# A two-layer encoder trunk on one core: x and mem also loaded transposed, the first norm scaled in after the first projection, keys and values of mem in one projection

## The chip, the cores and the metric

One core of a Trainium2 chip. The time is device microseconds (us) for one execution, as the median of several. The engines are named as the profile names them: PE is TensorE (PEld its weight loads), ACT is ScalarE, DVE is VectorE, POOL is GpSimd, SP is SyncE, which here issues every DMA, so that SP's order is the order of all loads.

## The reference

x is 256 tokens by 1024 features, mem is 256 by 1024, all f32. There are two layers, each a feed-forward block (FFN), a mixing block and a second FFN:

```python
h = rms_norm(x, ffn1_pre_g[l])
x = x + 0.5 * rms_norm(swiglu(h, ffn1_w_up[l], ffn1_w_down[l]), ffn1_post_g[l])
h = rms_norm(x, mix_pre_g[l])
u_pool, q_da, k_da, v_da, q_ca = jnp.split(h @ w_in[l], IN_SPLITS, axis=-1)
...
kv = rms_norm(mem, mem_norm_g[l]) @ w_mem_kv[l]
y_ca = memory_cross_attention(q_ca, kv)
...
x = x + rms_norm(merged @ w_out[l], mix_post_g[l])
h = rms_norm(x, ffn2_pre_g[l])
x = x + 0.5 * rms_norm(swiglu(h, ffn2_w_up[l], ffn2_w_down[l]), ffn2_post_g[l])
```

`rms_norm` divides each token's row by the root of its mean square and multiplies by a gain per feature; `swiglu` is `(silu(a) * b) @ w_down` with `a, b` the halves of `h @ w_up`. Each w_up has 2 x 2816 columns, each w_mem_kv 512 (256 for keys, 256 for values).

## The kernel before, in words

**Numbers.** A product in f32 is made of three matmuls on a split of each operand: a high part (fp32r, the rounded cast, on ACT) and a low part (the rest, on DVE). `mm3` (L201 to 209) issues high x high, high x low, low x high for each 128 features. Weights come as *units* of 128 x 2048 f32 (1 MiB). `load_unit` issues a unit's DMA into one of 3 raw buffers; `next_unit` (L105) casts it (ACT, L115) and makes its low part (DVE, L116) into one of 5 buffers. The first 5 units of a stage are split in 4 parts, later ones in 2.

**Tokens.** Two chunks c of 128 tokens. Activations that are multiplied stand transposed (features on partitions) in a tile `xhl`, high and low. `pre_norm` (L159) makes them: squares on ACT (L141) with a sum, DVE adds (L143), POOL raises to the power -0.5 (L134), DVE scales by 1/rms and gain, PE transposes eight 128 x 128 blocks (L182), ACT and DVE split them (L149, L150).

**An FFN** (L269) runs over 11 pairs of 256 hidden columns. Pairs 0 and 1 take the *wide* form: `up` with tokens as the stationary operand, 24 matmuls of 512 columns per chunk, then silu (L300), the product (L302), and two transposes per chunk (L307), which stand behind the next chunk's matmuls. Pairs 2 to 10 take the *narrow* form, `up2` (L314), with weights as the stationary operand; its result is already transposed, so it has no transposes. After pair p the down projection of pair p-2 follows (L249). Two units feed one wide pair, two feed one narrow pair, one feeds a down projection.

**Start of the program** (L713 to 727): load x chunk 0, the gain, unit 0, x chunk 1, units 1 and 2; 18 matmuls on zeros (`WARM`, L725); then `pre_norm` of chunk 0 with its transposes and of chunk 1; its transposes are placed behind the 20th matmul of the first `up`. The first FFN takes `(c, p)` in the order (0,0), (1,0), (0,1), (1,1).

**Memory tokens.** In the first FFN of each layer, after pair 4, `mem_norm` (L454) loads mem and normalizes it; its 16 transposes come with pair 6. In the mixing block keys are made by `form_a` (weights stationary) and values by `form_b` (tokens stationary), 48 matmuls of 256 columns each.

**Order.** The program is scheduled by the tile framework, in the order of the code with priorities by dependence; `issue_after` pins a few places, and the tables `T_...` tell which matmul of the mixing block's running list an attention step follows.

Of the kernel before, what the change touches and what calls it, by code (L numbers as in the profile page):

```python
# [17 lines left out]
P = 128  # L18
D = 1024
KT = D // P  # L20
S = 256
# [9 lines left out]
WARM = 18  # L31
T_FIRST = 19
# [4 lines left out]
T_DA = (275, 298, 341, 356)  # L37
T_PV = (282, 306, 349, 371)
T_LN = (321, 392)
T_CA = (412, 438)  # L40
T_CAV = (432, 442)
# [5 lines left out]
def encoder_kernel(ctx, tc, x_d, mem_d, pos_d, w_d, gains_d, cols_d, lamv_d, poolw_d, cst_d, out_d):  # L47
# [44 lines left out]
    first_xn = []  # L92
# [11 lines left out]
    def next_unit():  # L104
# [8 lines left out]
        for s in range(parts):  # L113
            cs = slice(s * n, (s + 1) * n)
            nc.scalar.copy(out=h[:, cs], in_=raw[:, cs])  # L115
            low = nc.vector.tensor_tensor(out=l[:, cs], in0=raw[:, cs], in1=h.bitcast(F32)[:, cs], op=ALU.subtract)  # L116
            if nxt[1] == 0:
                issue_after([low], first_xn[1])
# [13 lines left out]
    def rsqrt(v, n):  # L132
        r = sm(n)
        nc.gpsimd.tensor_tensor(out=r, in0=v, in1=mhalf[:, :n], op=ALU.pow)  # L134
        return r

    def rstd_of(halves, fold=1.0, between=None):
        s = sm(2)
        for i, h in enumerate(halves):
            junk = small.tile([P, 512], BF16, name="junk", bufs=2)  # L140
            nc.scalar.activation(out=junk, in_=h, func=AF.Square, scale=fold / 32.0, accum_out=s[:, i:i + 1])  # L141
# [4 lines left out]
        return rsqrt(v, 1)  # L146

    def split(ps, h, l):
        nc.scalar.copy(out=h, in_=ps)  # L149
        nc.vector.tensor_tensor(out=l, in0=ps, in1=h.bitcast(F32), op=ALU.subtract)  # L150
# [8 lines left out]
    def pre_norm(c, src, g, xx, direct=None):  # L159
# [8 lines left out]
        r = rstd_of(src, 1.0, None if direct else gained)  # L168
        for b in range(2):
            fs = slice(b * 512, (b + 1) * 512)  # L170
            if direct:
                first_xn.append(nc.vector.scalar_tensor_tensor(out=xn[:, fs], in0=src[b], scalar=r, in1=direct[b], op0=ALU.mult, op1=ALU.mult))
            else:
                nc.vector.tensor_scalar(out=xn[:, fs], in0=xn[:, fs], scalar1=r, scalar2=None, op0=ALU.mult)
# [26 lines left out]
    def mm3(out, pairs):  # L201
# [3 lines left out]
        for (ah, al), (bh, bl) in pairs:  # L205
            for lhsT, rhs in ((ah, bh), (ah, bl), (al, bh)):
                done.append(nc.tensor.matmul(out=out, lhsT=lhsT, rhs=rhs, start=(i == 0), stop=(i == n - 1)))  # L207
# [23 lines left out]

    def form_b2(out, lo, hi, c, xx):
        pairs = []
        for i, w in enumerate((lo, hi)):
            wh, wl = (t.rearrange("p (k m) -> p k m", k=4) for t in w)
            pairs += [((xx[0][:, c, 4 * i + k, :], xx[1][:, c, 4 * i + k, :]), (wh[:, k, :], wl[:, k, :])) for k in range(4)]
        return mm3(out, pairs)
# [31 lines left out]
    def ffn(i, xx, late, g_post, finish, ahead):  # L269
# [25 lines left out]
        def up(p, c, ws):  # L295
            ps = ma_bank()
            now = form_b2(ps, ws[0], ws[1], c, xx)
            flush()
            sg = t2((P, 2, P))
            nc.scalar.activation(out=sg, in_=ps[:, 0:256].rearrange("p (u m) -> p u m", u=2), func=AF.Silu)  # L300
            hn = t2((P, 2, P))
            nc.vector.tensor_tensor(out=hn, in0=ps[:, 256:512].rearrange("p (u m) -> p u m", u=2), in1=sg, op=ALU.mult)  # L302
# [9 lines left out]
            return now  # L312
# [16 lines left out]
        ws = [(next_unit(), next_unit()) for _ in range(2)]  # L329
        for p in range(2):  # L330
            hid_pair(p)
        done = []
        order = [(0, 0), (0, 1), (1, 0), (1, 1)] if i > 0 else [(0, 0), (1, 0), (0, 1), (1, 1)]
        for c, p in order:
            now = up(p, c, ws[p])
            done += now
            if len(done) == (48 if i > 0 else 24):
                issue_after(late, done[T_UP if i > 0 else T_FIRST])
        for p in range(2, NPR):
            hid_pair(p)  # L340
            for u in range(2):
                up2(p, u)
            if p - 2 <= NPR - 4:
                down(p - 2)
            if p == 4:
                turns = ahead()
            if p == 6:
                for t in turns:
                    t()
# [4 lines left out]
    colt = const.tile([P, DEPTH * 3], F32, name="colt")  # L354
# [8 lines left out]
    def setup():  # L363
        nc.sync.dma_start(out=cst, in_=cst_d)
        nc.sync.dma_start(out=colt, in_=cols_d)
# [70 lines left out]
    def lambdas():  # L436
        nc.scalar.activation(out=lamt, in_=lams, func=AF.Exp)
        for l in range(DEPTH):
            nc.vector.tensor_scalar(out=lamc[:, l:l + 1], in0=lamt[:, 2 * l:2 * l + 1], scalar1=lamt[:, 2 * l + 1:2 * l + 2],
                                    scalar2=lam_init[l], op0=ALU.subtract, op1=ALU.add)  # L440
            nc.vector.tensor_scalar(out=gsub[:, l:l + 1], in0=colt[:, l * 3 + 2:l * 3 + 3], scalar1=1.0 - lam_init[l], scalar2=None, op0=ALU.mult)
# [12 lines left out]
    def mem_norm(l):  # L454
        g = gain(l * 10 + 3)
        mm = xt_pair()
        turns = []
        for c in range(2):
# [5 lines left out]
            turns.append(pre_norm(c, m, g, mm))  # L464
        return mm, turns

    def mix(l, xx, late, mm, finish):
# [71 lines left out]
        w = next_unit()  # L539
        ps = ma_bank()  # L540
        for t in range(2):
            fill += form_a(ps[:, t * S:(t + 1) * S], w, slice(t * P, (t + 1) * P), mm)
        nc.scalar.copy(out=kc.rearrange("p t s -> p (t s)"), in_=ps)
        w = next_unit()
        ps = ma_bank()
        for c in range(2):
            fill += form_b(ps[:, c * 256:(c + 1) * 256], w, c, mm)
        nc.scalar.copy(out=vc.rearrange("p c m -> p (c m)"), in_=ps)
# [174 lines left out]
    wb = mb_bank()  # L723
    for _ in range(WARM):
        nc.tensor.matmul(out=wb, lhsT=warm[:, 0:P], rhs=warm, start=True, stop=True)  # L725
    pre_norm(0, halves(x[0]), None, cur, g0)()
    late = pre_norm(1, halves(x[1]), None, cur, g0)()
# [133 lines left out]
```

## Time and profile before

| what | value |
|---|---|
| median of 3 runs | 1154.98 us (1154.05 to 1155.45) |
| the profiled execution, span from first to last instruction | 1154.1 us |
| PE busy | 1141.8 us, 99% of the span |
| DVE, ACT, POOL busy | 768.6, 634.1, 28.6 us |
| DMA | 217.82 MB, 189 GB/s over the span |

The span is what the profile gives as this execution's own time; it is 0.9 us under the median of the runs. The profile names an instruction by its engine, its line in the kernel, what it writes and reads, and the number of instructions in a group. The chain of waits goes back from the last instruction to what released each step, so a stretch of it that is all PE is one in which PE alone sets the pace.

### The profile page before, as it was taken

How to read it: one execution, taken by the hardware profiler on the slowest of the kernel's cores; microseconds unless marked ns; L12 is line 12 of the kernel's file. 1: busy time of each engine (PE TensorE's matmuls, PEld its weight loads, DVE VectorE, ACT ScalarE, POOL GpSimd, SP SyncE). 2: the span in 40 equal slices, each digit the busy share in tenths (PEclk: the TensorE clock that was granted, in tenths of full speed). 3: DMA queues.
4: the chain of work that ended last, by engine and by line, in shares of the span. 5: the costliest groups of instructions: out<-in, count | busy, mean ns of one | idle time of the engine just before them, and what ended most of it. 6: DMA issues, size and time to landing. Idle time of an engine off the chain costs nothing.

```text
span 1154.1 us, 15241 instructions
## 1 busy us (share of the span) xinstructions
PE 1141.8 (99%) x5930; PEld 963.4 (83%) x5930; DVE 768.6 (67%) x1198; ACT 634.1 (55%) x1141; POOL 28.6 (2%) x39
## 2 busy tenths in 40 slices
PE   8999999999999999999999999999999999999997
PEld 5888888898888888888888888888978888888886
DVE  5768665665767876665586766675677678666653
ACT  5657554644665555555465655556455646555551
POOL 0000000000000100000000000010000001000000
PEclk8999999999999999999999999999999999999999
DMA  8865554564444575555456665535535544755530
GB/s 298 299 236 213 183 183 146 183 219 146 164 172 162 194 271 191 183 182 189 176 191 228 223 216 180 185 141 192 209 120 194 201 165 166 248 190 182 183 110 36
DMA packets 34055, 217.82 MB, mean 189 GB/s; under 512 B 4032, under 2 KB 4288, under 8 KB 9664
## 3 DMA queue, kind: packets, MB, share of 16 engines
q1 hardware_dynamic: 33984, 216.86, 53.0%
q8 instruction: 46, 0.75, 0.3%
q14 instruction: 25, 0.20, 0.0%
HBM read 215.80 MB, written 1.05 MB: 188 GB/s over the span
## 4 chain that ended last, share of the span: by engine, by line
PE 98%; DMA 1%; ACT 0%; SPq 0%; issue 0%; DVE 0%; DVEq 0%; POOLq 0%; ACTq 0%
PE ma L207 30%; PE acc L249 25%; PE mb L226 18%; PE ma L226 18%; PE mb L207 2%; PE mb L182 1%; PE acc L207 1%; PE acc L560 1%; DMA raw<-in_w 1%; PE mb L449 1%; PE acc L577 1%; PE acc L618 1%; PE acc L603 1%; PE mb L307 0%; PE mb L691 0%; PE mb L507 0%
## 5 line engine op out<-in xcount | busy, mean ns | idle before, releaser
L116 DVE TENSOR_TENSOR wl<-raw,wh 128x1024 fp32r<-128x1024 f32 (+1 forms) x444 | 460.2, 1077 | 140.2 <-ACT wh L115 125.9
L115 ACT CAST wh<-raw 128x1024 fp32r<-128x1024 f32 (+1 forms) x444 | 392.1, 935 | 169.8 <-issue 112.4
L207 PE MATMUL ma<-wh,xhl 128*128 128x512 f32 (+1 forms) x928 | 290.5, 390 | 1.9 <-ACT xhl L149 1.9
L249 PE MATMUL acc<-wh,hid 128*128 128x512 f32 x704 | 223.8, 390 | 0.0
L226 PE MATMUL ma<-xhl,wh 128*128 128x512 f32 x576 | 209.9, 399 | 0.0
L226 PE MATMUL mb<-xhl,wh 128*128 128x512 f32 x576 | 209.3, 398 | 0.0
L207 PEld LDWEIGHTS ma<-wh,xhl 128*128 128x128 f32 x928 | 172.8, 190 | 37.5 <-ACT xhl L149 2.2
L207 PE MATMUL ma<-wl,xhl 128*128 128x512 f32 (+1 forms) x464 | 180.2, 388 | 0.0
L249 PEld LDWEIGHTS acc<-wh,hid 128*128 128x128 f32 x704 | 132.2, 188 | 26.1
L226 PE MATMUL ma<-xhl,wl 128*128 128x256 f32 x576 | 150.1, 281 | 0.0
L226 PE MATMUL mb<-xhl,wl 128*128 128x256 f32 x576 | 150.1, 281 | 0.0
L249 PE MATMUL acc<-wl,hid 128*128 128x512 f32 x352 | 137.1, 389 | 0.0
L226 PEld LDWEIGHTS ma<-xhl,wh 128*128 128x128 f32 x576 | 108.2, 188 | 20.9
L226 PEld LDWEIGHTS mb<-xhl,wh 128*128 128x128 f32 x576 | 108.7, 189 | 19.2
L324 DVE TENSOR_TENSOR s<-mb,s 128x256 f32<-128x256 f32 x72 | 30.6, 425 | 130.2 <-ACT s L323 130.1
L226 PEld LDWEIGHTS mb<-xhl,wl 128*128 128x128 f32 x576 | 109.0, 189 | 6.6
L226 PEld LDWEIGHTS ma<-xhl,wl 128*128 128x128 f32 x576 | 108.8, 189 | 5.9
L207 PEld LDWEIGHTS ma<-wl,xhl 128*128 128x128 f32 x464 | 88.2, 190 | 17.3 <-issue 1.3
L249 PEld LDWEIGHTS acc<-wl,hid 128*128 128x128 f32 x352 | 66.2, 188 | 13.9
L325 ACT ACTIVATE s<-s 128x256 f32<-128x256 f32 x72 | 30.1, 418 | 69.5 <-DVE s L324 69.5
L323 ACT COPY s<-mb 128x256 f32<-128x256 f32 x72 | 26.8, 372 | 74.3 <-PE mb L226 74.3
L134 POOL TENSOR_TENSOR sm<-sm,mhalf 128x1 f32<-128x1 f32 (+1 forms) x32 | 27.9, 871 | 1119.8 <-DVE sm L143 855.2
(153 smaller groups left out, 991.3 us busy)
## 6 DMA issues: line engine op xcount, KB each, us to landing
raw<-in_w SPq DMA_DIRECT2D x190, 1024.0 KB, 4.9
gain<-in_gains SPq DMA_DIRECT2D x20, 512.0 KB, 5.2
raw<-in_w SPq DMA_DIRECT2D x4, 512.0 KB, 8.3
hid<-in_mem SPq DMA_DIRECT2D x8, 256.0 KB, 6.0
x<-in_x SPq DMA_DIRECT2D x4, 256.0 KB, 6.3
out<-x SPq DMA_DIRECT2D x4, 256.0 KB, 2.1
cst<-in_cst SPq DMA_DIRECT2D x1, 304.0 KB, 5.3
pw<-in_poolw SPq DMA_DIRECT2D x2, 128.0 KB, 4.0
```

What stands on the lines that cost most here:

```text
L115: nc.scalar.copy(out=h[:, cs], in_=raw[:, cs])
L116: low = nc.vector.tensor_tensor(out=l[:, cs], in0=raw[:, cs], in1=h.bitcast(F32)[:, cs], op=ALU.subtract)
L134: nc.gpsimd.tensor_tensor(out=r, in0=v, in1=mhalf[:, :n], op=ALU.pow)
L182: tps.append(nc.tensor.transpose(out=ps[:, k * P:(k + 1) * P], in_=xn[:, i * P:(i + 1) * P], identity=ident))
L207: done.append(nc.tensor.matmul(out=out, lhsT=lhsT, rhs=rhs, start=(i == 0), stop=(i == n - 1)))
L226: nc.tensor.matmul(out=o, lhsT=ww[:, k, ms], rhs=rhs, start=(k == 0 and o is full), stop=(k == KT - 1 and o is full))
L249: done.append(nc.tensor.matmul(out=banks[b], lhsT=a, rhs=ww[:, k, fs], start=(kk == first and k == 0 and i == 0), stop=(kk == last and k = ...
L323: nc.scalar.copy(out=half, in_=banks[i][:, S:2 * S])
L324: nc.vector.tensor_tensor(out=half, in0=banks[i][:, 0:S], in1=half, op=ALU.add)
L325: nc.scalar.activation(out=t[:, 0:S], in_=t[:, 0:S], func=AF.Silu)
L449: ins.append(nc.tensor.transpose(out=tp[:, i * P:(i + 1) * P], in_=a[:, hh, kt * P:(kt + 1) * P], identity=ident))
L560: nc.tensor.matmul(out=banks[m][:, hh * S:(hh + 1) * S], lhsT=qT[rs, c, 2 * hp + hh, :], rhs=kT[rs, :, 2 * hp + hh, :], start=True, stop=True)
```

## The change

The host also gives x and mem transposed. The first FFN of layer 0 splits raw x^T, times the gain, straight from the load (no norm, no transposes ahead of its matmuls); 1/rms of each token, computed beside, is applied where the projection is read out of PSUM, in silu's scale and in the product. That needs tokens on partitions, so all 11 pairs of this FFN take the wide form. mem^T times its gain is split in the same way; 1/rms of mem is computed once, for both layers, and applied where the keys and values are read out. Keys and values are one wide projection, and the keys are transposed afterwards, two blocks per chunk.

```diff
-WARM = 18
+WARM = 11
...
-T_DA = (275, 298, 341, 356)
+T_DA = (227, 250, 293, 308)
...
+    def gained_split(out, src, col):
+        high = nc.scalar.activation(out=out[0], in_=src, func=AF.Copy, scale=col)
+        return high, nc.vector.scalar_tensor_tensor(out=out[1], in0=src, scalar=col, in1=out[0].bitcast(F32), op0=ALU.mult, op1=ALU.subtract)
...
+        def up_first(p, ws):
+            banks = [ma_bank(), ma_bank()]
+            for i, w in enumerate(ws):
+                for c in range(2):
+                    mm3(banks[c], half_b(w, i, c, xx), i == 0, i == 1)
+            for c in range(2):
+                swiglu(p, c, banks[c])
...
+            if raw_rstd:
+                nc.scalar.activation(out=sg, in_=gate, func=AF.Silu, scale=raw_rstd[c])
+                nc.vector.scalar_tensor_tensor(out=hn, in0=value, scalar=raw_rstd[c], in1=sg, op0=ALU.mult, op1=ALU.mult)
...
+        if raw_rstd:
+            hs, ls = first_high, first_low
+            (ha, la), (hb, lb), (hc, lc), (hd, ld) = (zip(*late[c, b]) for b in range(2) for c in range(2))
+            in_order([*ha, *hs[0:4], *hb, *hc, hs[4], hs[5], *hd, *hs[6:8]])
+            in_order([*la, *ls[0:4], *lb, *lc, ls[4], ls[5], *ld, *ls[6:8]])
+            ws.append((next_unit(), next_unit()))
+            for c in range(2):
+                rstd_of(halves(x[c]), 1.0, None, raw_rstd[c])
...
-            for u in range(2):
-                up2(p, u)
+            if raw_rstd:
+                w2 = (next_unit(), next_unit())
+                for c in range(2):
+                    up(p, c, w2)
+            else:
+                for u in range(2):
+                    up2(p, u)
...
-    def mem_norm(l):
...
+    def mem_gain(l):
+        mm = xt_pair()
+        for b in range(4):
+            t = hids.tile([P, 2, 2, P], F32, name="hid")
+            nc.sync.dma_start(out=t, in_=memt_d[:, b * 512:(b + 1) * 512].rearrange("p (k c t) -> p k c t", k=2, c=2))
+            for i in range(2):
...
+                gained_split((mm[0][:, :, k, :], mm[1][:, :, k, :]), t[:, i], colt[:, col:col + 1])
...
-            fill += form_a(ps[:, t * S:(t + 1) * S], w, slice(t * P, (t + 1) * P), mm)
-        nc.scalar.copy(out=kc.rearrange("p t s -> p (t s)"), in_=ps)
...
+            now = form_b2(ps, ws[0], ws[1], c, mm)
...
+            nc.scalar.activation(out=kt.rearrange("p t d -> p (t d)"), in_=ps[:, 0:S], func=AF.Copy, scale=rmem[:, c:c + 1])
+            nc.vector.tensor_scalar(out=vc[:, c, :], in0=ps[:, S:2 * S], scalar1=rmem[:, c:c + 1], scalar2=None, op0=ALU.mult)
...
-    load_x(0)
-    g0 = halves(gain(0))
-    load_unit(2)
-    load_x(1)
-    load_unit(2)
-    load_unit()
+    xt = {(0, 0): load_tokens(0, 0)}
+    nc.sync.dma_start(out=colt, in_=cols_d)
+    load_unit(4)
+    xt[1, 0] = load_tokens(1, 0)
+    xt[0, 1] = load_tokens(0, 1)
+    load_unit(4)
+    xt[1, 1] = load_tokens(1, 1)
+    load_unit(2)
+    for c in range(2):
+        load_x(c)
```

`half_b` is one unit's half of `form_b2`; `mem_scale` (once) loads mem and computes its 1/rms.

The change moves instructions at the start. ACT before, from its first instruction (`s_271` and `s_305` are silu's outputs, `hid<-mb` the first split of the hidden tile):

```order
1 L413 ACT_TABLE_LOAD
2 L413 ACTIVATE sm<-mhalf 128x1
3 L141 ACTIVATE junk,sm<-x_91 128x512 x2
4 L115 CAST wh<-raw 128x512 x4
5 L149 CAST xhl<-mb 128x512 x2
6 L141 ACTIVATE junk,sm<-x_92 128x512 x2
7 L115 CAST wh<-raw 128x512 x6
8 L149 CAST xhl<-mb 128x512 x2
9 L115 CAST wh<-raw 128x512 x2
10 L300 ACTIVATE s_271<-ma 128x256
```

and ACT now, from the same place (`hid<-in_xt` tiles hold x^T, `rst` is 1/rms):

```order
3 L165 ACTIVATE xhl<-hid,colt 128x128 x4
4 L114 CAST wh<-raw 128x512 x4
5 L165 ACTIVATE xhl<-hid,colt 128x128 x8
6 L114 CAST wh<-raw 128x512 x2
7 L165 ACTIVATE xhl<-hid,colt 128x128 x4
8 L114 CAST wh<-raw 128x512 x6
9 L145 ACTIVATE junk,sm<-x_91 128x512 x2
10 L145 ACTIVATE junk,sm<-x_92 128x512
11 L330 ACTIVATE s_299<-ma,rst 128x256
12 L145 ACTIVATE junk,sm<-x_92 128x512
13 L330 ACTIVATE s_303<-ma,rst 128x256
14 L154 CAST hid<-mb 128x256 x2
```

The squares of x moved from ahead of every weight cast to behind the casts of units 0, 1 and 2, and no split waits for a transpose any more. All of this feeds from SP, whose first rows now are these (20 DMAs stand ahead of unit 3, which is the first of those of `128x2048`; `x_91` and `x_92` are the two chunks of x):

```order
1 L170 DMA hid<-in_xt 128x512
2 L773 DMA colt<-in_cols 128x30
3 L99 DMA raw<-in_w 128x512 x4
4 L170 DMA hid<-in_xt 128x512 x2
5 L99 DMA raw<-in_w 128x512 x4
6 L170 DMA hid<-in_xt 128x512
7 L99 DMA raw<-in_w 128x1024 x2
8 L83 DMA x_91<-in_x 128x512 x2
9 L83 DMA x_92<-in_x 128x512 x2
10 L87 DMA gain<-in_gains 128x1024
11 L99 DMA raw<-in_w 128x2048 x10
```

Before, x and the gain came first, and units 0 to 2 in five pieces; what moved is that x now lands behind unit 2. The third place is ACT around the memory tokens in the first FFN, now (`lamt`, `snd` and `csd` are small constants; `s_881` is silu's output for chunk 0 of pair 5):

```order
40 L145 ACTIVATE junk,sm<-hid 128x512 x2
41 L482 ACT_TABLE_LOAD
42 L482 ACTIVATE lamt<-lams 128x4
43 L145 ACTIVATE junk,sm<-hid 128x512 x2
44 L165 ACTIVATE xhl<-hid,colt 128x2x128
45 L451 ACT_TABLE_LOAD
46 L451 ACTIVATE snd<-turns 128x2x8
47 L452 ACTIVATE snd<-turns 128x2x8
49 L165 ACTIVATE xhl<-hid,colt 128x2x128 x7
50 L154 CAST hid<-mb 128x256
51 L330 ACT_TABLE_LOAD
52 L330 ACTIVATE s_881<-ma,rst 128x256
```

Before, the four squares and the table loads there stood between weight casts and silus; now they and the eight splits of mem^T stand in one piece ahead of pair 5's silu.

## Rows read from the trace of the kernel before

**Rows 1.** The page: busy time by engine, and the granted clock in 40 slices.

```profile
PE 1141.8 (99%) x5930; PEld 963.4 (83%) x5930; DVE 768.6 (67%) x1198; ACT 634.1 (55%) x1141; POOL 28.6 (2%) x39
...
PEclk8999999999999999999999999999999999999999
```

**Rows 2.** The chain of waits, 0 to 60 us: start, us, what.

```profile
2.59 8.47 DMA raw<-in_w
...
12.75 7.68 PE ma L207 x20
...
21.31 6.37 PE ma L207 x28
...
33.60 5.50 PE ma L207 x24
39.10 0.22 PE mb L307 x2
39.32 2.83 PE ma L226 x16
...
50.83 5.45 PE acc L249 x24
```

**Rows 3.** Windows: us, busy (x instructions) of PE, PEld, DVE, ACT, POOL, granted clock, DMA.

```profile
5.00:10.00 5.00, 2.79 (x14) 1.25 (x12) 1.58 (x3) 0.94 (x3) 0.55 (x1) 1.00 0.96 326
12.00:15.00 3.00, 2.25 (x5) 1.78 (x6) 2.27 (x5) 3.00 (x9) 0.18 (x1) 0.51 1.03 433
...
18.00:20.00 2.00, 2.00 (x8) 1.60 (x7) 2.00 (x4) 0.55 (x2) 0.00 (x0) 0.78 0.83 320
20.00:25.00 5.00, 5.00 (x27) 4.21 (x27) 4.29 (x9) 4.09 (x9) 0.00 (x0) 1.00 0.64 231
```

**Rows 4.** Timeline, 0 to 27 us: start, us, engine, line, operation, count, idle before.

```profile
1.19 6.04 PE L725 MATMUL mb<-s 128*128 128x512 bf16 x18 [1.19 <-DVE up L530]
...
3.45 0.63 ACT L141 ACTIVATE junk<-x 128x512 bf16<-128x512 f32 x1 [1.22 <-DMA x<-in_x]
...
5.34 1.39 PEld L725 LDWEIGHTS <-s 128*128 128x128 bf16 x7 [0.19 <-issue]
...
14.31 2.17 ACT L115 CAST wh<-raw 128x512 fp32r<-128x512 f32 x4
...
14.82 0.93 POOL L134 TENSOR_TENSOR sm<-sm,mhalf 128x1 f32<-128x1 f32 x1 [7.94 <-DVE sm L143]
...
24.27 2.49 DVE L116 TENSOR_TENSOR wl<-raw,wh 128x512 fp32r<-128x512 f32 x4
```

**Rows 5.** DMA of 0 to 20 us: GB/s in 40 slices of 0.5 us, and the sum.

```profile
GB/s 0 0 0 82 336 250 344 201 225 201 221 270 360 377 320 360 344 303 303 397 414 401 414 389 442 442 410 467 426 410 393 426 352 279 205 328 377 344 393 164
DMA packets 1709, 6.19 MB, mean 309 GB/s; under 512 B 186, under 2 KB 186, under 8 KB 1466
```

**Rows 6.** The tile x, 0 to 20 us: its four loads of 256 KiB, issue to landing.

```profile
DMA to landing us min/median/max: 2.7/6.3/8.6
```

**Rows 7.** The chain of waits, 84 to 140 us.

```profile
100.99 5.45 PE acc L249 x24
...
117.71 5.45 PE acc L249 x24
...
136.32 3.86 PE acc L249 x17
```

**Rows 8.** Timeline of PE, mixing block: first and last of 48 matmuls of one projection.

```profile
256.17 0.28 PE L207 MATMUL ma<-wh,xhl 128*128 128x256 f32 x1
...
261.81 0.28 PE L207 MATMUL ma<-wh,xhl 128*128 128x256 f32 x1
```

**Rows 9.** Lines 643 and 644, scaled splits: ns min/median/max, first and last start.

```profile
L643 ACT ACTIVATE xhl<-mb,colt x4: 463/469/476, 334.6 to 902.2; 128x256 fp32r<-128x256 f32 x4
L644 DVE SCALAR_TENSOR_TENSOR xhl<-mb,colt,xhl x4: 483/484/485, 335.1 to 902.7; 128x256 fp32r<-128x256 f32 x4
```

**Rows 10.** Timeline of ACT, 84 to 97 us: one of three table loads.

```profile
89.36 1.28 ACT L437 ACT_TABLE_LOAD   x1
```

More of the change, by code (lines that the diff above doesn't have):

```diff
@@ L30 @@
 QSCALE = 64 ** -0.5
-WARM = 18
-T_FIRST = 19
+WARM = 11
 FINE = 5
@@ L130, in issue_after, with in_order, rsqrt, rstd_of @@
                               reason="issue order")
-    def rsqrt(v, n):
-        r = sm(n)
+    def in_order(ins):
+        for early, late in zip(ins, ins[1:]):
+            issue_after([late], early)
+    def rsqrt(v, n, r=None):
+        r = sm(n) if r is None else r
         nc.gpsimd.tensor_tensor(out=r, in0=v, in1=mhalf[:, :n], op=ALU.pow)
         return r
-    def rstd_of(halves, fold=1.0, between=None):
-        s = sm(2)
+    def rstd_of(halves, fold=1.0, between=None, into=None, listed=False):
+        s, sq = sm(2), []
         for i, h in enumerate(halves):
             junk = small.tile([P, 512], BF16, name="junk", bufs=2)
-            nc.scalar.activation(out=junk, in_=h, func=AF.Square, scale=fold / 32.0, accum_out=s[:, i:i + 1])
+            sq.append(nc.scalar.activation(out=junk, in_=h, func=AF.Square, scale=fold / 32.0, accum_out=s[:, i:i + 1]))
         v = sm(1)
@@ L199, in post_norm, with mm3 @@
             nc.vector.scalar_tensor_tensor(out=x[c][:, fs], in0=ts[b], scalar=r, in1=x[c][:, fs], op0=ALU.mult, op1=ALU.add)
-    def mm3(out, pairs):
+    def mm3(out, pairs, first=True, last=True):
         n = 3 * len(pairs)
@@ L206, in mm3 @@
             for lhsT, rhs in ((ah, bh), (ah, bl), (al, bh)):
-                done.append(nc.tensor.matmul(out=out, lhsT=lhsT, rhs=rhs, start=(i == 0), stop=(i == n - 1)))
+                done.append(nc.tensor.matmul(out=out, lhsT=lhsT, rhs=rhs, start=(first and i == 0), stop=(last and i == n - 1)))
                 i += 1
@@ L230, in form_b, with half_b @@
         return mm3(out, [((xx[0][:, c, k, :], xx[1][:, c, k, :]), (wh[:, k, :], wl[:, k, :])) for k in range(KT)])
+    def half_b(w, i, c, xx):
+        wh, wl = (t.rearrange("p (k m) -> p k m", k=4) for t in w)
+        return [((xx[0][:, c, 4 * i + k, :], xx[1][:, c, 4 * i + k, :]), (wh[:, k, :], wl[:, k, :])) for k in range(4)]
     def form_b2(out, lo, hi, c, xx):
[L233 to L237, printed above, removed]
+        return mm3(out, half_b(lo, 0, c, xx) + half_b(hi, 1, c, xx))
     def rows_chunk(c, banks, todo, lhs_of, first, last):
@@ L267, in tail, with ffn @@
         return tps
-    def ffn(i, xx, late, g_post, finish, ahead):
+    def ffn(i, xx, late, g_post, finish, ahead, raw_rstd=None):
         fine[0] = FINE
@@ L345, in ffn @@
             if p == 4:
[L346 to L349, printed above, removed]
+                ahead()
         todo = [(next_unit(), p) for p in range(NPR - 3, NPR)]
@@ L745, in ahead @@
                     setup()
+                    mem_scale()
                 if row == 0:
-                    nx["mem"], turns = mem_norm(l)
-                    return turns
-                return []
-            late = ffn(i, cur, late, gain(l * 10 + row + 1), finish, ahead)
+                    nx["mem"] = mem_gain(l)
+            late = ffn(i, cur, late, gain(l * 10 + row + 1), finish, ahead, [rst[:, c:c + 1] for c in range(2)] if i == 0 else None)
         else:
@@ L811, in _pack @@
             cols(wi, slice(s, s + 256))
-        for s in (0, 256):
-            cols(a["w_mem_kv"][l], slice(s, s + 256))
+        wide(a["w_mem_kv"][l], slice(0, 512))
         for i in range(6):
```

126 lines of the change are left out of this document (73 added, 53 removed).

## The prediction

> **What bounds the kernel now.** I read the page first: PE is busy 1141.8 of the 1154.1 us, DVE 768.6, ACT 634.1, and PE's granted clock is full in every slice but the first [rows 1]. So a change pays only by what it takes out of PE's own list, or out of the first microseconds, where PE is not yet fed. The chain of waits from 0 to 60 us then shows the start: a wait for the raw weights, the first real matmul at 12.75, the first two pairs done at 39.32, pair 2 done at 50.83 [rows 2]. These two pairs are 96 matmuls; at 5.45 us for 24, which is 0.227 each [rows 2], they should take 21.8 us, and took 26.6 with the transposes among them. The reason stands in the windows: PE was busy 2.8 of the 5 us from 5 to 10, and from 12 to 15 the granted clock was 0.51 [rows 3], which is the 1.2 GHz level; from 20 on it is full, 2.4 GHz. The eighteen warm matmuls had ended at 7.2 and PE waited for x, the gain and the transposes. After that PE alone sets the pace: the steady period of a narrow pair with its down projection is 117.71 - 100.99 = 16.72 us [rows 7], all of it PE. The sum below is made against the span of 1154.1; the median of the runs is 0.9 higher, so the forecast adds 0.9.
>
> **Term A, the start.** What must come in before pair 1 can end is now 26 pieces of 256 KiB up to and with unit 3 (4 of x^T, 4 for each of four units, 4 of x, 2 of the gain): 6.8 MB. Before, 6.19 MB moved in the first 20 us, of which the first 1.6 or so were idle [rows 5]: 338 GB/s. At this pace unit 3 is complete at 1.6 + 20.2 = 21.8, and about 0.7 for the landing (x's first piece, with 0.8 us of transfer, was used 2.7 after its issue [rows 4, 6]) makes 22.5.
>
> PE starts far earlier. x^T's first piece lands at 3.4, as x's did [rows 4]. ACT then splits four blocks of 128 columns. No row shows that size; a scaled split costs 469 ns on ACT and 484 on DVE at 256 columns [rows 9], and back to back the casts go at 2.17 / 4 = 0.54 and the low parts at 2.49 / 4 = 0.62 us per 512 columns [rows 4], so I take 0.3 us each. The first weight quarter is then cast at about 5.4, and the eleventh warm matmul ends there too (seven of the eighteen load their weights after 5.34 [rows 4]): PE goes from warm to real work with no gap, at full clock. Feeding it for units 0 to 2 is 16 blocks and 12 quarters, 11.3 us on ACT and 12.2 on DVE, against 48 + 24 matmuls or 16.3 us on PE; so PE sets the pace, with waits of some 0.5 us. Pair 0 ends at about 16.7.
>
> Now the new waits. Pair 0's silu needs 1/rms of x, and x lands behind unit 2: 20 pieces, 5.2 MB, about 17.8. Squares (0.63 and a read of 0.2 each), DVE's sum and POOL's 0.93 [rows 4] put the two scales at about 19.2 and 21.3. Two transposes of chunk 0 stand after 12 matmuls of unit 2, those of chunk 1 five matmuls later; PE stalls about 1 us at each and is at the end of unit 2 near 24.2. All that is behind them on ACT (the first split of the hidden tile, then unit 3's casts) waits too, but unit 3 landed only at 22.5, so this costs nothing more. Its four quarters are paced by DVE (2.49) to 26.2; eleven more matmuls and a transpose pair end pair 1 at about 29.4. Before: 39.32. **A = -9.9.** Unit 4 lands some 2.6 later, unit 5 another 2.6 (1 MiB at the 400 GB/s of the later slices [rows 5]), and both are split before PE wants them at 29.4 and 32.1. Bounds: PE without any wait from 5.4 on would end pair 1 at 5.4 + 21.8 + 0.7 = 27.9, -11.4. At the slowest slices of the start [rows 5] unit 3 would land at 32.5 (225 GB/s) or 36.1 (201), and pair 1 end at 39.4 or 43.0: 0 to +3.7. I take the mean pace, because the slow slices fall in the time when the gain was read, which now comes last.
>
> **Term B, nine pairs in the wide form.** A wide chunk is 5.50 + 0.22 = 5.72 us with its two transposes [rows 2], a pair 11.44; a narrow pair is 16.72 - 5.45 = 11.27 [rows 2, 7]. Eight pairs cost 0.17 more each; pair 2 took 11.51 with a leftover transpose [rows 2] and now takes 11.44. **B = +1.3.** What comes free, four evacuation steps per pair on ACT and DVE, was beside PE and is worth nothing.
>
> **Term C, mem's transposes.** The period with them was 136.32 - 117.71 = 18.61, so 16 transposes cost 1.89 [rows 7]; there are two such layers. **C = -3.8.** The norm's DVE work that goes was hidden. The splits of mem^T, eight on each of ACT and DVE in each layer at 0.4 to 0.5 [rows 9], replace four larger ones and hide under PE too.
>
> **Term D, keys and values.** 96 matmuls of 256 columns start every (261.81 - 256.17) / 47 = 0.12 us [rows 8], 11.5 us; 48 of 512 columns take 10.9. The four key transposes give 0.44 back (0.22 a pair [rows 2]). **D = -0.4** for both layers, between -1.3 (transposes free) and +0.9 (each pair late once by half a microsecond); each waits for a read of PSUM that has 13 matmuls, 3 us, to cover it.
>
> **Term E, the memory block on ACT.** In the first FFN four squares, three table loads of 1.28 [rows 10] and eight splits now stand in one piece before pair 5's first silu: 4 x 0.72 + 3 x 1.28 + 8 x 0.39 and six small ones make 11.4 us, 14.2 with the silu and the casts ahead of them since the end of pair 4's matmuls. From there PE comes to the transposes that need pair 5's silu in 16.8 us (transposes 0.44, a down projection and two chunks of 5.45). With 0.5 for DVE's product the cover is 2 us, so **E = 0**, and +2 if it is gone. On SP the loads of mem and mem^T queue behind a small load that waits for pair 3's last transposes, and two of mem^T behind the first squares; the next weight unit behind them is not wanted for 20 us.
>
> **Sum.** -9.9 + 1.3 - 3.8 - 0.4 + 0 = -12.8: 1141.3 for the profiled execution, 1142.2 beside the median. **I forecast 1142.**
>
> **A rule against it.** The loads of the start are cut from halves of 512 KiB into quarters of 256. The rows say that this does no harm: x's four pieces of that size flew beside others, the fastest landing in 2.7 us [rows 6], at a mean of 309 GB/s for all [rows 5]. The Trainium skill (DMA: Bandwidth & Descriptors, section Bandwidth) says to batch to a MiB or more for three quarters of the peak, with about 2 us fixed for each DMA; paid one after the other, this would be an estimated 2.6 us for each of some 16 pieces, and the change would lose. The trace does not agree as long as several are in flight, as here.
>
> **The rivals.** (1) *The clock falls at the start.* If PE's small waits let it fall as the waits of 5 to 10 us did before, from about 12 to about 18.9 [rows 3], half of these 6.9 us is lost: pair 1 ends at 32.9, A = -6.4, in all 1145.7. If it does not rise at all until 18.9, 30 matmuls are done by then at twice 0.227, and 66 more with 0.7 of transposes end pair 1 at 34.6: 1147.4. For it: the same engine, the same place. Against: PE now has work through the whole of that time, where before it was busy 2.8 us of five [rows 3]. (2) *The memory block stalls PE.* If mem's loads, which wait in SP's queue, land several microseconds late, each microsecond over the 2 of cover is one of PE: with 6 late, +4, about 1146. For: everything stands in one chain. Against: before, the same squares and table loads stalled nothing. (3) *Slower than before.* The small pieces do not fly side by side. If each is paid alone, 16 of 2.7 us [rows 6] bring unit 3 no sooner than 45, pair 1 ends past 52, and the kernel takes about 1165. It decides from where A exceeds the 2.9 us that the rest saves: pair 1 ending after 42.2, unit 3 landing after 35, a pace under 206 GB/s; to be slower by over 0.2% (2.3 us, about what a measurement of this kernel can tell from no change) under 193. The slowest half-microseconds of the start are 201 [rows 5], with the gain's broadcast among them. (4) *The start gains nothing*: x^T comes sooner, but units 2 and 3 come behind 1 MB of x, and PE only waits elsewhere. That is the pace of 206 to 225 GB/s, A about 0 to +2.9, in all 1152 to 1155.
>
> **How the numbers follow.** The forecast has 0.64, the clock 0.18, the memory block 0.10, (4) and (3) 0.04 each. The range goes from the full start gain with free key transposes (-11.4 - 3.8 - 1.3 + 1.3 = -15.2, so 1139.8; 1139 with the spread of the runs) to the clock rival's later end with a stall of 2 us and the spread of the runs on top, 1150. The first three cases lie in it but for their tails: 8 in 10. Faster 0.92, same 0.04, slower 0.04.
>
> **What would show it.** Right: the first wide matmul at 5 to 6 us, full clock from there, pair 1 ended at 28 to 31, unit 3's casts soon after 22.5; no L182 transposes in the two stretches of mem, their period at pair 6 back to the ordinary one; 11.4 us for every pair of the first FFN; one projection of 10.9 us for keys and values. Wrong: a clock of 0.5 after 12 us (rival 1), an idle PE before the transposes of pair 5 (rival 2), casts of units 2 and 3 that wait for their DMA beyond 25 us (rivals 3 and 4).

## The result, and the profile after

The changed kernel takes **1144.11 us** (median of 4 runs, 1143.92 to 1144.51), the kernel before 1154.91 (1154.05 to 1155.45) beside it: ratio 0.9907, 95% interval 0.9893 to 0.9921, 10.8 us less. The forecast was 1142 in a range of 1139 to 1150: right, with the gain taken 2 us too large.

The page of the changed kernel, its line of busy times and its granted clock by 40 slices, to be set beside [rows 1]:

```profile
PE 1133.2 (99%) x5679; PEld 947.5 (83%) x5679; DVE 752.0 (66%) x1164; ACT 626.8 (55%) x1121; POOL 25.4 (2%) x37
...
PEclk9999999999999999999999999999999999999999
```

PE is still the bound and lost 8.6 us of busy time. The other 3.0 us of the 11.6 between the two profiled executions are idle time: PE's waits at the start are 3.0 us in place of 5.3, and the end of the span, told below, is 0.6 shorter. The chain of waits of the changed kernel, 0 to 60 us (start, us, what), answers to [rows 2]:

```profile
1.65 4.33 DMA raw<-in_w
...
6.01 0.63 ACT wh L114
...
7.41 12.49 PE ma L222 x47
19.90 2.72 PE acc L222 x12
22.62 0.22 PE mb L339 x2
22.84 1.16 PE acc L222 x5
24.00 0.22 PE mb L339 x2
24.22 7.09 PE acc L222 x31
...
31.53 5.47 PE ma L222 x24
...
42.91 5.47 PE acc L264 x24
...
59.74 0.46 PE acc L264 x2
```

PE feeds itself without a break from 7.41; pair 0 ends at 19.90, pair 1 at 31.53, where before it ended at 39.32. The two pairs of transposes (L339 at 22.62 and 24.00) follow the products with no wait between. From pair 2 on a pair with its down projection takes 59.74 - 42.91 = 16.83 us, against 16.72 in the narrow form [rows 7].

By windows (us; busy time and instructions of PE, PEld, DVE, ACT, POOL; granted clock; DMA) the start of the changed kernel, beside [rows 3]:

```profile
5.00:10.00 5.00, 3.16 (x8) 2.30 (x8) 3.60 (x10) 3.71 (x10) 0.00 (x0) 0.73 0.95 321
10.00:12.00 2.00, 2.00 (x8) 1.59 (x8) 1.92 (x9) 2.00 (x7) 0.00 (x0) 0.81 1.05 405
12.00:15.00 3.00, 3.00 (x15) 2.46 (x14) 2.31 (x6) 1.95 (x6) 0.00 (x0) 1.00 1.03 412
```

PE is full from 10 us on, at full clock from about 10.6. Between 5 and 12 the clock was partly at its lower level, 1.2 GHz. The timeline of PE, changed kernel, 0 to 12 us, shows where (start, us, operation, count, idle before):

```profile
1.19 3.88 PE L786 MATMUL acc<-s 128*128 128x512 bf16 x11 [1.19 <-DVE up L583]
6.68 0.49 PE L222 MATMUL ma<-wh,xhl 128*128 128x512 f32 x1 [1.61 <-ACT wh L114]
...
8.00 1.05 PE L222 MATMUL ma<-wh,xhl 128*128 128x512 f32 x2
...
9.28 1.05 PE L222 MATMUL ma<-wh,xhl 128*128 128x512 f32 x2
```

The warm matmuls end at 5.07, PE is idle for 1.6 us, and then three products take 9.28 - 8.00 = 1.28 us, 0.43 each, where 0.227 is the full rate.

**Stage by stage**, from the chains of both profiles (before, then after). The first transposes at the end of the first FFN stand there as

```profile
200.76 0.87 PE mb L182 x8
192.10 0.87 PE mb L197 x8
```

Pair 1 ended at 39.32, now at 31.53, -7.8. From there to the first transposes at the end of this FFN (200.76, now 192.10) -0.9, which is +1.0 for the wide form and -1.9 for mem's transposes. Layer 0's mixing block and its second FFN's start -0.2; mem's stretch in layer 1 -1.9; layer 1's mixing block -0.2. All else is within 0.1, but for the time from the last vector operation to the end of the span, 3.65 us before and 3.03 now: -0.6. This last piece is 2.9 to 3.7 us in the profiles of this study, whatever the edit (3.6 with 43 warm matmuls in the kernel before, 3.5 with the new start alone, 3.0 with the memory part alone), and nothing here shows what sets it, so it is not counted as won by the change. Together -11.6, the difference of the two spans (1154.1, 1142.5).

One reading misleads. In the mixing block the chain of the changed kernel leaves PE for DVE and ACT; this is its stretch from 265 to 270 us:

```profile
265.71 1.11 PE acc L617 x8
266.83 1.28 DVE sm L466 x2
...
269.49 1.13 PE acc L617 x4
```

That looks like a stall of 2.7 us, new with the change. But PE's own timeline has scores to 267.6 and products from there to 269.45: the chain only follows the releaser that came last, by a hair. The summary of PE's waits, whole program (total, times, longest), names no such wait:

```profile
PE ma L222 <- ACT wh L114: 1.6, 1, 1.6
PE acc L786 <- DVE up L583: 1.2, 1, 1.2
PE ma L222 <- DVE wl L115: 0.2, 1, 0.2
```

### The profile page after: what moved, and what is told of

Same layout as the page of the kernel before. It is cut to its first block, busy times and chain, and to the rows that moved or that the text cites. A ratio compares the mean times of both kernels' runs of the same rounds, so it can differ in the third digit from the quotient of the medians.

```text
span 1142.5 us, 14737 instructions
## 1 busy us (share of the span) xinstructions
PE 1133.2 (99%) x5679; PEld 947.5 (83%) x5679; DVE 752.0 (66%) x1164; ACT 626.8 (55%) x1121; POOL 25.4 (2%) x37
## 4 chain that ended last, share of the span: by engine, by line
PE 98%; DVE 0%; DMA 0%; ACT 0%; issue 0%; SPq 0%; DVEq 0%; POOLq 0%; ACTq 0%
PE ma L222 37%; PE acc L264 25%; PE mb L241 13%; PE ma L241 13%; PE acc L222 2%; PE mb L222 2%; PE mb L197 1%; PE acc L617 1%; PE mb L339 1%; PE mb L495 1%; PE acc L634 1%; PE acc L675 1%; PE acc L660 1%; DMA raw<-in_w 0%; PE mb L748 0%; PE mb L560 0%
## 5 line engine op out<-in xcount | busy, mean ns | idle before, releaser
L222 PE MATMUL ma<-wh,xhl 128*128 128x512 f32 x1184 | 379.6, 395 | 1.6 <-ACT wh L114 1.6
L222 PEld LDWEIGHTS ma<-wh,xhl 128*128 128x128 f32 x1184 | 221.9, 189 | 49.0 <-ACT wh L114 2.1
L222 PE MATMUL ma<-wl,xhl 128*128 128x512 f32 x592 | 233.1, 394 | 0.2 <-DVE wl L115 0.2
L241 PE MATMUL ma<-xhl,wh 128*128 128x512 f32 x432 | 157.4, 398 | 0.0
L241 PE MATMUL mb<-xhl,wh 128*128 128x512 f32 x432 | 157.0, 397 | 0.0
L241 PE MATMUL mb<-xhl,wl 128*128 128x256 f32 x432 | 112.5, 281 | 0.0
L241 PE MATMUL ma<-xhl,wl 128*128 128x256 f32 x432 | 112.4, 281 | 0.0
L241 PEld LDWEIGHTS mb<-xhl,wh 128*128 128x128 f32 x432 | 81.5, 189 | 14.5
L241 PEld LDWEIGHTS mb<-xhl,wl 128*128 128x128 f32 x432 | 81.6, 189 | 5.0
L241 PEld LDWEIGHTS ma<-xhl,wl 128*128 128x128 f32 x432 | 81.5, 189 | 4.6
L138 POOL TENSOR_TENSOR sm<-sm,mhalf 128x1 f32<-128x1 f32 (+1 forms) x26 | 22.5, 865 | 1029.7 <-DVE sm L147 836.9
```

The costliest lines, as they stand in the source:

```text
L241: nc.tensor.matmul(out=o, lhsT=ww[:, k, ms], rhs=rhs, start=(k == 0 and o is full), stop=(k == KT - 1 and o is full))
```

## The experiments

"Pair 1 ends" is read from the chain of each run's profile, as above; three profiles with the same start end it at 30.93, 31.53 and 31.71, so the times are given beside it. The kernel before, run beside each group, took 1154.89, 1155.25 and 1155.40 us.

### The parts alone

Start alone: the new start and wide first FFN, with the memory path of before.

```diff
-                    mem_scale()
...
-                    nx["mem"] = mem_gain(l)
+                    nx["mem"], turns = mem_norm(l)
...
-        wide(a["w_mem_kv"][l], slice(0, 512))
+        for s in (0, 256):
+            cols(a["w_mem_kv"][l], slice(s, s + 256))
```

Expected: 

> The start of the change alone (x given transposed, first FFN wide with 1/rms at the evacuation); mem is normed and turned on TensorE, and keys and values are two projections, as before. If the parts simply add, as the chains of the two profiles say (start -7.8, wide form +1.0): span 1147.3, time about 1148.1 (1154.9 - 6.8). Rival (the parts lean on each other, the memory block costs the start something): anything outside 1147 to 1149.

Measured: 1149.53 us, ratio 0.9954 [0.9939, 0.9969], above the 1147 to 1149 expected; span of the profiled run 1147.3, as expected, pair 1 ends at 31.46. The profiled run's time was 1149.09, 1.8 above its span, where the expectation had added 0.8: so most of the miss is the way from span to time and not the parts.

Memory part alone: the converse edit, made to the kernel before.

Expected: 

> The memory part of the change alone: mem given transposed, 1/rms of mem at the evacuation, one projection for keys and values; the start and the first FFN as before. If the parts add (transposes -3.8, projection -0.3): time about 1150.8 (1154.9 - 4.1), pair 1 ending at 39.3 as before. Rival: the transposes of the keys or the block of squares hold TensorE in the narrow first FFN, and the time is 1152 or more.

Measured: 1151.74 us, ratio 0.9972 [0.9961, 0.9982], between theory and rival; profiled span 1150.4, pair 1 ends at 40.16. The old start scatters: its two waits of PE, for the scaled x and for the split of what was turned, are 2.6 and 2.2 us here, 2.2 and 1.9 in the profile of before.

What follows: both parts pay. Behind pair 1 the two profiles nearly add up: start alone needs 1112.3 us from there to its last vector operation, memory alone 1107.2, before 1111.1, so +1.2 and -3.9; the changed kernel 1107.9, which is -3.2 where the parts give -2.7. The kernel before with 43 warm matmuls, below, needs 1111.5 for this stretch, so 0.4 of scatter is in the old kernel itself. In the medians the parts give -5.4 and -3.2, 8.5 of the 10.8; with intervals of 1.2 to 1.7 us each this neither shows nor excludes that they help each other, and it stays open.

### The warm matmuls, the gap and the clock

```diff
-WARM = 11
+WARM = 18
```

Expected: 

> After with WARM = 18 in place of 11; nothing else. In the profile of the changed kernel the eleven warm matmuls end at 5.07 us, TensorE then has nothing for 1.6 us, the first weight product starts at 6.68, its successors stand 0.43 us apart until 10.56 and 0.227 apart from there on; pair 1 ends at 31.53. Theory (the gap): the 1.6 us without work cost the fast rate; with seven more warm matmuls (7 x 0.227 = 1.6) the gap is closed, the real ones run 0.227 apart from the first, chunk 0 of unit 0 ends about 1.4 us sooner, and pair 1 ends 0.9 to 1.4 us sooner, at 30.1 to 30.6 (the second transposes have 0.95 us in hand before 1/rms of chunk 1 holds them). Time about 1143.0. Rival (feeding): the 0.43 us is the pace of the casts and subtractions; then the spacing stays, pair 1 ends at 31.5 and the time is 1144.1.

Measured: 1144.41 us, ratio 0.9913 [0.9898, 0.9927]: no gain. From the start of the first product to that of the eighth it is 2.3 us on PE's timeline, against 3.5 in the changed kernel. The chain shows why pair 1 ended no sooner, at 31.52:

```profile
21.70 0.57 POOL rst L138
22.29 0.48 ACT s L330
...
22.80 0.50 DVE s L331
...
23.34 0.44 PE mb L339 x2
23.78 7.52 PE acc L222 x33
```

The gap theory was right about the rate and wrong about the end: PE came earlier and now waited 0.6 us for chunk 1's 1/rms; between, the products were held to the pace of the casts. The edit also moved something that the expectation does not have: the schedule put these transposes behind 63 products in place of the 65 of the changed kernel (33 products stand behind them in this chain, 31 there), so 0.45 us of work that could have filled the wait stood behind it.

```diff
-WARM = 11
+WARM = 1
```

Expected: 

> After with WARM = 1; nothing else, so TensorE has almost no work before the first real product at 6.7 us. Theory (the gap undoes what the warm matmuls did): the real ones run 0.43 us apart from 6.7 to some 9.6 to 10.6 as they do with eleven warm ones, pair 1 ends at 31.2 to 32.0, time 1144 plus or minus 0.5. Rival (the warm matmuls still help in spite of the gap): the slow spacing lasts longer than in the changed kernel, pair 1 ends at 33 or later, time over 1145.5.

Measured: 1144.98 us, ratio 0.9916 [0.9901, 0.9931]; the products stand 0.43 apart from 7.78 to 10.35, pair 1 ends at 32.34. The lower level lasted no longer than with eleven warm matmuls that are followed by a gap, yet the run was 0.9 us slower. The chain shows a reason that is not the clock:

```profile
23.48 0.44 PE mb L339 x2
...
23.92 8.20 PE acc L222 x36
```

Here the schedule put chunk 1's transposes behind 60 products in place of 65. PE waited 0.6 us for 1/rms, and 36 products were left, 5 more than in the changed kernel, 1.1 us at 0.227. The squares had started 0.6 us later as well. So the run is between the two theories and prices the warm matmuls no better than the last one: in both, the order changed with the number.

The changed kernel once more: 

> The changed kernel once more, as it is, beside the two that follow. If the moment at which the warm matmuls go over to the fast rate varies from run to run (4.05 us in the profile of the changed kernel, 4.15 and 6.28 in those with WARM = 18), the gap before the first product is 0.5 to 1.6 us here and pair 1 ends at 31.4 to 31.6 all the same, since the transposes wait for 1/rms or nearly so. Time 1143.9 to 1144.5.

Measured: 1143.79 us (1143.71 to 1143.86), ratio 0.9901 [0.9886, 0.9915]. Pair 1 ends at 30.93, 0.6 sooner than in the first profile, and sooner than I allowed. Its weight loads (timeline of PEld) show another rate:

```profile
5.00 0.15 PEld L786 LDWEIGHTS <-s 128*128 128x128 bf16 x1 [0.28 <-issue]
6.04 0.19 PEld L222 LDWEIGHTS ma<-wh,xhl 128*128 128x128 f32 x1 [0.89 <-ACT wh L114]
```

Beside it, PEld of the run with WARM = 18 and late transposes, told below:

```profile
5.86 0.15 PEld L792 LDWEIGHTS <-s 128*128 128x128 bf16 x1 [0.28 <-issue]
6.28 0.96 PEld L792 LDWEIGHTS <-s 128*128 128x128 bf16 x5 [0.28 <-issue]
```

A single load each 0.43 us is the slow rate, five in 0.96 the fast one. In the first profile the warm matmuls went over to the fast rate at about 4.1 us, finished early, left 1.6 us idle and the products then ran slowly until 10.6; here they were slow to their end or nearly so, PE was idle for 0.3 us, and the products were fast as soon as nothing held them (two in 0.47 from 8.31). So the slow stretch in my profile is not a fixed price of eleven warm matmuls; it differs from one execution to the next. The 0.6 us is not all the clock's either: the first cast came 0.6 us sooner here, at 5.38, and PE then waited 0.4 us for chunk 1's 1/rms.

Two things could decide it: the moment at which the rate changes, which differs by itself, and the length of the gap. In the run of the start alone, with the same eleven warm matmuls, these were slow to their end too, but the gap was 0.8 us, and its timeline of PE goes on

```profile
6.85 0.79 PE L222 MATMUL ma<-wh,xhl 128*128 128x512 f32 x1 [0.79 <-ACT wh L114]
...
9.45 1.03 PE L222 MATMUL ma<-wh,xhl 128*128 128x512 f32 x2
```

with the products 0.43 us apart until 10.3. With x loaded ahead, below, the gap was 0.5 and the products were fast. Which of the two decides stays open.

### What holds pair 1 once the clock is right

Both chunks go through unit 2, then come pair 0's transposes, then unit 3, whose casts now stand ahead of the split of the hidden tile.

```diff
-WARM = 11
+WARM = 18
...
+                if i == 0:
+                    for turn in pending:
+                        issue_after(turn(), now[-1])
+                    pending.clear()
...
+                if raw_rstd and p == 0:
+                    issue_after([done[0]], first_high[15])
+                    issue_after([done[1]], first_low[15])
...
-            for c in range(2):
-                up(1, c, ws[1], acc_bank)
+            up_first(1, ws[1], acc_bank)
```

Expected: 

> After with WARM = 18 and another order of pair 1: both chunks through unit 2 (24 products), then pair 0's two transposes, then both chunks through unit 3; unit 3's four casts and subtractions stand ahead of the split of the turned hidden tile on ScalarE and VectorE. With WARM = 18 alone the fast rate came from the first product, yet pair 1 ended at 31.52 as before, because the transposes of chunk 1 waited for 1/rms until 23.34 and unit 3's casts stood behind the split of what they turned. Theory (1/rms of chunk 1 is the next limit): with the transposes behind 24 products, which end near 23.5, nothing waits, unit 3 is cast from about 22.3, and pair 1 ends at 29.3 to 30.2; time 1142.2 to 1143.0. Rival (unit 3's transfer is the next limit): its casts begin at 24 or later all the same, pair 1 ends at 31 to 31.5, and the time is that of the changed kernel.

Measured: 1143.39 us (1143.31 to 1143.80), ratio 0.9897 [0.9882, 0.9912]. The chain, start to pair 2:

```profile
1.19 6.56 PE acc L792 x18
7.75 11.01 PE ma L222 x48
18.76 5.44 PE acc L222 x24
24.20 0.44 PE mb L342 x4
24.64 5.49 PE acc L222 x24
30.13 5.44 PE ma L222 x24
```

Nothing waits any more: 96 products in 21.9 us, and pair 1 ends at 30.13, 1.4 sooner than in the first profile of the changed kernel and in the one with WARM = 18 alone. The end is inside the theory's range, the time 0.4 above it. 1/rms of chunk 1 was the next limit, and unit 3's transfer was not: ACT's timeline has its first cast behind a silu and with no wait for the DMA.

```profile
22.35 2.19 ACT L114 CAST wh<-raw 128x512 fp32r<-128x512 f32 x4
```

The edit moves the transposes and the split of the hidden tile together, so the run does not tell what each is worth.

What is left is the warm matmuls, which ran past the first cast, ready at 6.6. With WARM = 15:

Expected: 

> The late transposes of pair 0 as before (both chunks through unit 2, then the transposes, then unit 3, whose casts come first), with WARM = 15 in place of 18, since the eighteen warm matmuls ended at 7.75 there and the first cast had been ready at 6.6. Theory: the first product starts at 6.7, the products are paced by the casts up to some 10 us, pair 1 ends at 29.4 to 30.1; time 1142.7 to 1143.4. Rival (unit 3 or the pace of the casts holds it): pair 1 ends at 30.1 to 30.6, time 1143.4 or more.

Measured: 1143.28 us (1143.00 to 1143.81), ratio 0.9897 [0.9882, 0.9911]; pair 1 ends at 30.66 in the profiled run. There the warm matmuls stayed slow until about 7.1, and the cast of unit 0's last quarter waited for its DMA until 8.74: the time fits the theory, the profile the rival.

And with x loaded ahead of unit 2 besides:

```diff
-    load_unit(2)
     for c in range(2):
         load_x(c)
+    load_unit(2)
```

Expected: 

> As the run with late transposes and WARM = 15, and with x loaded ahead of unit 2. Theory (with everything else out of the way 1/rms of chunk 1 still holds unit 3's casts back on ScalarE, behind a silu that starts at 21.9): x 2.6 us sooner brings the silu to about 20 and pair 1 ends at 29.2 to 29.8; time 1142.5 to 1143.1. Rival (unit 2 comes too late, four squares stand ahead of two of its quarters): pair 1 ends at 30 to 30.8, time 1143.4 to 1144.1.

Measured: 1143.98 us, ratio 0.9903 [0.9888, 0.9918], pair 1 ends at 30.76: the rival. The four squares stand ahead of two of unit 2's casts, and the chain goes through the last of those, at 18.26. The same edit in the changed kernel as it is:

Expected: 

> After with the loads of x moved ahead of unit 2 on SyncE's queue (WARM = 11). Theory: in the changed kernel nothing waits for 1/rms, so that x 2.6 us sooner (1 MiB at some 400 GB/s) is worth nothing, and unit 2 is what comes later: its first quarter is wanted by TensorE at 19.9, and with four squares (2.6 us) ahead of its casts on ScalarE pair 1 ends between 31.5 and 33; time 1144.0 to 1145.5. Rival (the scales hold the start): pair 1 ends sooner than 31, time below 1143.7.

Measured: 1144.21 us, ratio 0.9905 [0.9889, 0.9922], pair 1 ends at 30.84. The time is the theory's, the end of pair 1 the rival's, sooner than 31 us; it is also that of the changed kernel's second profile, so this run decides nothing beyond the time.

The versions with late transposes are the fastest of the study, 0.4 and 0.5 us below the changed kernel's second measurement; that is under what a measurement tells apart here.

### The size of the first pieces

```diff
-    load_unit(4)
+    load_unit()
```

(units 0 and 1)

Expected: 

> After with units 0 and 1 loaded as one transfer of 1 MiB each in place of four of 256 KiB. Theory (the small pieces fly side by side, and their use is that the first one is there early): the first quarter can be cast only when the whole unit is there, at 7.5 to 8.5 in place of 6.01, and pair 1 ends 1 to 2.5 us later, at 32.5 to 34; time 1145 to 1146.6. Rival (each transfer has a fixed price, as the rule on batching has it): six fewer transfers bring the units sooner, pair 1 ends before 31.5, and the time is below 1144.

Measured: 1146.12 us (1145.28 to 1147.42), ratio 0.9921 [0.9906, 0.9936], 2.0 to 2.3 us slower than the changed kernel; pair 1 ends at 34.61, past the theory's range. The four runs lie apart (1145.28, 1145.34, 1146.91, 1147.42), and the profiled one is the slowest. ACT's timeline:

```profile
8.58 2.18 ACT L114 CAST wh<-raw 128x512 fp32r<-128x512 f32 x4 [3.52 <-DMA raw<-in_w]
```

The first cast starts 2.6 us later than the 6.01 of the changed kernel, and pair 1 ends 3.1 later than in its first profile: PE's products, 0.43 us apart at first in both, are so until 14.4 here and 10.6 there, so a part of the loss is the clock's. DMA of 0 to 20 us, changed kernel:

```profile
DMA packets 2954, 6.39 MB, mean 320 GB/s; under 512 B 448, under 2 KB 448, under 8 KB 2880
```

and with whole units:

```profile
DMA packets 2119, 6.61 MB, mean 331 GB/s; under 512 B 354, under 2 KB 354, under 8 KB 1762
```

The larger transfers move 3% more per second (the versions with small pieces have 310 to 322 GB/s), and lose all the same, because nothing can be cast before a whole unit is there. The Trainium skill (DMA: Bandwidth & Descriptors, section Bandwidth) lists higher rates for larger transfers, measured there on DMAs that the GpSimd issues, and the trace agrees in the direction (331 against 320 GB/s); what decides here is when the first piece can be cast. The 2 us fixed for a DMA, in the prediction's rule, stand in another section of that page of the Trainium skill (DMA: Bandwidth & Descriptors, section Anatomy of one DMA), for the same path; no run here shows them for DMAs that SP issues. The kernel before was not run with smaller first pieces, so it is open how much of the new start's gain they would have brought without x^T.

### The memory block's cover

```diff
-            rstd_of(m, 1.0, None, rmem[:, c:c + 1])
+            for _ in range(2):
+                rstd_of(m, 1.0, None, rmem[:, c:c + 1])
```

Expected: 

> After with the squares of mem taken twice (the second pass writes the same scales): four more squares of 0.7 us on ScalarE in the memory block ahead of pair 5's first silu, nothing more to load. In the profile of the changed kernel that silu ends at 91.44, the product that follows takes 0.5, and TensorE comes to the transposes that need it at 93.01: the cover left is 1.1 us. Theory (the block is hidden with 1.1 us to spare): 2.8 - 1.1 = 1.7 us of stall before pair 5's first transposes, pair 5's period 16.83 + 1.7 = 18.5, time 1145.8. Rival (the cover is bigger than that, since ScalarE has 1.4 us of waits for VectorE inside the block): no stall, period 16.8, time 1144.1.

Measured: 1145.66 us, ratio 0.9916 [0.9900, 0.9933], 1.9 above the changed kernel beside it; of the 2.1 between the two profiled spans 0.8 is the start (pair 1 ends at 31.71 here, at 30.93 there). The chain, 42 to 150 us:

```profile
59.92 5.47 PE acc L264 x24
...
93.61 0.48 ACT s L330
94.11 0.49 DVE s L331
94.74 0.41 PE mb L339 x2
...
111.76 5.47 PE acc L264 x24
```

Three pairs took 51.84 us, against 3 x 16.83 = 50.49: 1.35 came through. ACT's silu of this pair started 2.5 us later than in the changed kernel, set against the end of pair 1, so the four squares cost 2.5 and not 2.8, and the cover is 1.1 us, as read from the first profile: the theory holds, with its squares taken 0.3 too long.

### The old start with more warm matmuls

```diff
-WARM = 18
+WARM = 43
```

(in the kernel before)

Expected: 

> Before with WARM = 43 in place of 18, so that the warm matmuls run on until the first real product at about 12.8 us; nothing else. Theory (a good part of what the old start lost was the slow rate after the idle stretch from 7.2 to 12.75, not the transfers): the products run 0.227 apart from the first, at most half of the 6.1 us from 12.75 to 18.9 comes back, less what the transposes then wait for, and pair 1 ends at 36 to 38.5 in place of 39.3; time 1152 to 1154. Rival (the feed sets the old start): pair 1 ends at 39.3, time 1154.9.

Measured: 1157.25 us, ratio 1.0020 [1.0010, 1.0029]; pair 1 ends at 40.48. PE's timeline:

```profile
3.72 8.83 PE L725 MATMUL mb<-s 128*128 128x512 bf16 x37
12.39 1.04 PE L182 MATMUL mb<-ident,s 128*128 128x128 f32 x8
15.37 0.50 PE L207 MATMUL ma<-wh,xhl 128*128 128x512 f32 x1 [1.94 <-ACT xhl L149]
```

The products ran fast, but the transposes that stand behind the warm matmuls came at 12.39 in place of 9.44, and all that depends on them came later. Neither theory: the run does not price the clock of the old start, and shows only that warm matmuls up to the first product, all ahead of the transposes, cost more there than they give.

## Why the prediction was right, by its steps

**Term A** was given as -9.9 and came out at -7.8 between the two profiles: the direction and the parts were right, and this is the term that was mis-sized. The transfers were sized well. ACT squared x from 17.64 without a wait for its DMA (given: landed at 17.8), and unit 3 could be cast by 22.35 at the latest, in the run with late transposes (given: 22.5). The reason for taking the mean pace did not hold, though: the slowest half-microseconds, 176 and 102 GB/s from 3.5 to 4.5 us, are still there with the gain loaded last.

Three steps were off. The first product was to start at 5.4 and started at 6.68, since the first cast began only at 6.01: the first quarter took 4.3 us from its issue, with other pieces in flight. "PE goes from warm to real work with no gap, at full clock" failed: PE was idle for 1.6 us in one profile and 0.3 in the other, and in the first one the products ran slowly until 10.6, so pair 0 ended at 19.9, not at 16.7. Against that the two waits for 1/rms, taken at about 1 us each, did not come, because PE was late; in the runs where PE was on time one of them did (0.6 and 0.4 us). So -9.9 was near what the start can give, 30.1 us with the order mended being -9.2, but not with the order as it stood. Of the signs named for being right, the first product at 5 to 6 us, the full clock from there, pair 1 ended by 31 and unit 3's casts soon after 22.5 (24.52) were all missed in the first profile.

**Rival 1**, the clock, had a mechanism that is seen, but not its place: the clock fell in the first profile, and behind the idle stretch after the warm matmuls (products slow from about 7.4 to 10.6), not behind small waits from 12 to 18.9; from 12 to 15 the granted clock was 1.00. The rival took 3.5 us from term A, where 2.1 are missing in all. The changed kernel's second profile, without slow products, is 0.6 better, part of it by an earlier first cast; so the two profiles show no more than that for the clock, since the casts and 1/rms held PE in its place.

**Term B**, +1.3, measured +1.0: a wide chunk takes 5.44 to 5.47 us, not 5.50, and the pairs 0.11 more than narrow ones, not 0.17. **Term C**, -3.8: -1.9 in each layer. **Term D**, -0.4 for both layers: -0.3. **Term E**, 0: every period of the first FFN is 16.82 or 16.83 us, so rival 2 is out, but the cover is 1.1 us and not 2: inside the block ACT waits 0.58 and 0.78 us for small vectors of DVE, which the sum of its own work did not have. **Rivals 3 and 4** fell with the end of pair 1, 31.53 against the 42.2 from which the change would lose: the pieces did fly side by side (mean 320 GB/s over the first 20 us), and behind its first product PE waits for no transfer.

**The sum** of the terms as measured is -10.9, against -12.8. The two spans are 11.6 apart all the same, by the 0.6 at the end of the span that no term had and that scatters from profile to profile: there the forecast was helped by luck. The other step that failed was to add 0.9 for the way from span to median. In the runs beside the experiments the spans of before are 1152.2 to 1154.3 with times 1.8 us above them, those of the changed kernel 1141.7 to 1142.5 with times 2.0 above. The profile of before with its 1154.1 was thus an execution of about 1155.9, a microsecond slower than the median. With the 2.0 that the changed kernel turned out to have, the forecast would have been 1143.3, 0.8 from the median.

## What to carry to other kernels

Where PE is 99% busy, find the microseconds in which it is not yet fed, and see in what order pieces of data become usable: a norm taken out of the way of the first product and 256 KiB pieces for the first weights were together worth more here (7.8 us) than the matmuls and transposes that were removed (4.1); of the two only the pieces were tested apart, at 2.0 to 2.3 us. When one wait is taken away at the start, look for what is ready only just in time behind it (here 1/rms, 0.95 us ahead), since the next gain ends there. And set a profile's span against spans, not against the times of other runs.

## What the runs showed of the hardware that was not expected

In ten profiles, those of the changed kernel and its variants with eleven or more warm matmuls, these start alike at 1.19 us, 0.43 us apart. They go over to the full rate at about 4.1 us in four of them and at 6.3 to 7.1 in three; in the other three, with eleven warm matmuls, they are slow to their end or nearly so. Of the four that changed at 4.1 us, three had PE idle behind the warm matmuls, for 1.5, 1.6 and 4.1 us; in these the granted clock fell again between 7 and 8 us, and the products behind ran at the lower level until about 10.6 (14.4 with whole units). The fourth, with eighteen warm matmuls, had no idle stretch, and its granted clock stayed at 1.00. The Trainium skill (TensorE: Matmul & The Clock Gate, section Part 1: The HAM clock gate) says that the number of slow matmuls at a start varies from run to run; the runs agree, with 7 to some 14 of them. The granted clock of the window from 0 to 5 us reads 1.00 in all of these profiles, and in the run of the start alone also from 5 to 12, though its products stand 0.43 us apart until 10.3. So until the rate has changed for the first time the spacing of the matmuls, and not that column, tells their rate.
